# A two-level fast matrix product on one core: x loaded as fp16 by casting transfers from GpSimd, and one pair of additions moved to GpSimd

## The chip, the core and the metric

The kernel runs on one core of a Trainium2 chip. The core has five engines with instruction queues of their own: TensorE (PE, with its weight loads listed apart as PEld), VectorE (DVE), ScalarE (ACT), GpSimd (POOL) and SyncE (SP), which here only starts transfers. Each engine works through its queue strictly in order, and waits at an instruction until all that it depends on is done. The metric is the device time of the whole program in microseconds (us), median of the runs shown.

## The reference

```python
def reference(x, w):          # x: 8 x 2048 x 2048 float32, w: 2048 x 2048 float32
    cs = np.cumsum(x, axis=1)
    diff = cs - np.concatenate([zeros(8, 1, 2048), cs[:, :-1, :]], axis=1)
    return np.matmul(diff, w).astype(np.float32)
```

The difference of a running sum is x again, so what is computed is `x @ w`, with x seen as 16384 rows of 2048 numbers drawn from a normal distribution.

## The kernel before, in words

**Tiles and products.** The 128 row tiles of x (128 rows each) are numbered t. The first four (`PLAIN`) are multiplied in the plain way while w comes in. The others go in groups of four tiles, g to g+3 (g and h = g+2 give the upper blocks, g+1 and h+1 the lower ones), and a Strassen-like scheme with seven products instead of eight is used twice, one inside the other. w is held in SBUF as fp16 (its four blocks, and four combinations T1 to T4). There are 31 groups: `group_plain` for the first, `group` for the other thirty. A group's products are P1 and P2 (for C11), P5 (S1 with T1), the two direct ones `S2 T2` and `S3 T3`, which add up in the PSUM pairs X and Y, and P3 and P4. P1 to P5 are each split again into seven quarter products, `slot(0)` to `slot(6)` in the class `Quarters`. A quarter product needs sums of quarters of x: `s1`, `s2`, `s4` on DVE and `s3` on POOL. They are kept in two rooms, so `s3` overwrites `s1`, and has to wait until the product with `s1` (slot 1) is through. Slot 4 multiplies `s3`.

**How x comes in.** A tile comes as two halves of 128 x 1024 float32, by transfers that SP starts (`load`, L123) into four stage buffers F. ACT sums the magnitudes of each half (`weigh`, L133). From the two sums POOL makes the mean (L157), DVE its reciprocal (L159), and POOL the factor that undoes the scaling (`unit`, L160). ACT scales the halves to fp16 (`narrow`, L165), over the place of the first one. SP then starts two transposing transfers (`turn`, L185) into the x tiles that TensorE reads; a stage buffer is given back to the list after its narrow or its turn.

**How results go out.** ACT copies a PSUM bank into an SBUF buffer with the row's factor (`keep`, L561 to L568), DVE adds further banks to it (`add`, L573 to L579), and SP stores it (`put`, L582). X, once `S3 T3` is in it, goes into two results: `keep C21g` copies it, and `C22g+X` adds it to C22g, which already holds P5's part. The same holds for Y with C21h and C22h. Then P4 is added to C21 (`C21g+P4.g`, `C21h+P4.h`).

**What sets the order.** Every instruction is recorded with a label, an engine and a period (the group's number). The table `places` gives each label a due time inside its period of 2168 units, and `emit` (L197) issues all of them sorted by that time. So the table fixes the order of each engine's queue. Its entry `None` holds for the groups in the middle. In it, the end of a group has, in units: `keep C21g.0` 826, `keep C21g.1` 832, `C22g+X.0` 884, `keep C21h.0` 910, `C22h+Y.0` 989, `C22g+X.1` 990, `load8.0` 1057, `keep C21h.1` 1118, `load8.1` 1159, `C22h+Y.1` 1162, then the next group's `P1.s3` at 1213 (-955 of its own period) and `P2.s3` at 1426. `P4.s3` stands before them at 711, `load7.0` and `load7.1` at 790 and 818. ("load8" is the tile g+4 of the next group, by the number that it has in this one.)

Of the kernel before, what the change touches and what calls it, by code (L numbers as in the profile page):

```python
# [10 lines left out]
def kernel(  # L11
# [50 lines left out]
    tiny = const.tile([P, 64], f32, name="tiny")  # L62
    sums_at = [tiny[:, ds(2 * i, 2)] for i in range(4)]
# [14 lines left out]
    def area(kb, size, dtype):  # L78
        return arena[:, ds(kb * 256, size * 256)].bitcast(dtype) if dtype != f32 else arena[:, ds(kb * 256, size * 256)]
# [22 lines left out]
        last[engine] = said[-1] if isinstance(said, tuple) else said  # L102

    where = {}
    stage = [F[:, i, :] for i in range(4)]
    unit = {}
    sums_of = {}
    scales = {}
# [5 lines left out]
    def record(label, engine, ask):  # L114
        at = seen[period[0], label] = seen.get((period[0], label), 0) + 1
        if at > 1:
            label = f"{label}#{at}"
        ops.append((period[0], label, engine, ask))

    def role(t):  # L120
        return t - PLAIN - 4 * period[0]

    def load(t, i):  # L123
        if t < END:
            to = stage.pop(0)
            where.setdefault(t, [None, None])[i] = to
            record(
                f"load{role(t)}.{i}",
                "sp",
                lambda: nc.sync.dma_start(to, x2[ds(t * P, P), ds(i * NH, NH)]),  # L130
            )

    def weigh_one(t, i):  # L133
        m, data = sums_of[t][:, i : i + 1], where[t][i]
        record(
            f"weigh{role(t)}.{i}",
            "act",
            lambda: nc.scalar.activation(waste, data, ABS, scale=1.0 / ROW, accum_out=m),  # L138
        )

    def weigh(t, sides=range(2)):
        if t < END:
            if t not in sums_of:
                sums_of[t] = sums_at[t % 4]
            for i in sides:
                weigh_one(t, i)

    def scale_of(t):
        if t < END:
            m2 = sums_of.pop(t)  # L150
            m = means_at[t % 4]
            s = scales[t] = scales_at[t % 8]
            u = unit[t] = units_at[t % 8]
            record(
                f"mean{role(t)}",
                "pool",
                lambda: nc.gpsimd.tensor_scalar(m, m2[:, :1], m2[:, 1:], TINY, ADD, MAX),  # L157
            )
            record(f"scale{role(t)}", "dve", lambda: nc.vector.reciprocal(s, m))  # L159
            record(f"unit{role(t)}", "pool", lambda: nc.gpsimd.tensor_scalar(u, m, uw, None, MUL))  # L160

    def narrowed(t):
        return where[t][0].bitcast(f16)

    def narrow_one(t, i):  # L165
        to, data, s = narrowed(t)[:, ds(i * NH, NH)], where[t][i], scales[t]
        record(
            f"narrow{role(t)}.{i}",
            "act",
            lambda: nc.scalar.activation(to, data, COPY, scale=s),  # L170
        )
        if i == 1 and t != PLAIN + 1:
            stage.append(where[t][1])

    def narrow(t, sides=range(2)):
        if t < END:
            for i in sides:
                narrow_one(t, i)

    turns_left = {}  # L180

    def place(t):
        return turned_x[(t - PLAIN) // 2 % 2 + 2 * (t % 2)]

    def turn_one(t, i):  # L185
        to, data = place(t)[i], narrowed(t)[:, ds(i * NH, NH)]
        record(f"turn{role(t)}.{i}", "sp", lambda: nc.sync.dma_start_transpose(to, data))
        turns_left[t] = turns_left.get(t, 2) - 1
        if turns_left[t] == 0 and t != PLAIN + 1:
            stage.append(where[t][0])  # L190

    def turn(t, halves=range(2)):
        if t < END:
# [1 line left out]
                turn_one(t, i)  # L195

    def emit(places=None):  # L197
        def when(op):
# [254 lines left out]
    weigh(PLAIN + 2)  # L453
    scale_of(PLAIN + 2)
    finish_row(1)
    x5 = area(30, 8, f32)
    where[PLAIN + 1] = [x5[:, :NH], x5[:, NH:]]
    for i in range(2):

        def load_5(i=i):  # L460
            return nc.sync.dma_start(
                x5[:, ds(i * NH, NH)], x2[ds((PLAIN + 1) * P, P), ds(i * NH, NH)]
            )

        record(f"load1.{i}", "sp", load_5)
    put_done()
    narrow(PLAIN + 2)
    turn(PLAIN + 2)
# [292 lines left out]
    def group_plain(g):  # L761
        X, Y, Z, V = pairs
        h = g + 2
        ug, uh, vg = unit[g], unit[h], unit[g + 1]
        A11g, A12g = parts(g)
        A11h, A12h = parts(h)
        A21g, A22g = parts(g + 1)
# [24 lines left out]
        turn(h + 1)  # L792
        load(h + 4, 0)
        less("T2[4:]", T2[4:], B22[4:], T1[4:])
        vh = unit[h + 1]
# [88 lines left out]
    def group(g):  # L884
# [9 lines left out]
        ug, uh, vg, vh = (unit[t] for t in (g, h, g + 1, h + 1))  # L894
# [241 lines left out]
    period[0] += 1  # L1136
    ready["tail"]()


    places = {  # L1140
        0: {
# [493 lines left out]
    }  # L1635
    emit(places)


# [1 line left out]
_INS = ['x', 'w']  # L1640
# [26 lines left out]
```

## Time and profile before

| What | Value |
|---|---|
| median of two runs | 1456.43 us (1455.78 to 1457.09) |
| span of the profiled execution | 1457.7 us |
| DVE, ACT, POOL busy | 1245.1, 1132.1, 288.1 us |
| DMA share in the middle, 700 to 744 us | 0.88 |
| one load of 128 x 1024 float32, start to landing, median over the run | 5.5 us |
| one transposing transfer, the same | 3.7 us |

The profile gives the profiled execution its span, from the first to the last instruction, and no other time; the span is 1.27 us above the median of the runs. Engine rows of a timeline read: start, duration, engine, source line, operation, output <- inputs, count, and in brackets the idle time before it and what ended it. A line such as L520 is that of a helper and stands for many uses; the operands and the time tell them apart. Rows with SPq are transfers as SP issues them, not as they move.

### The profile page before, as it was taken

Reading aid. Unit: us, or ns where it says so; the run is one execution under the profiler, and the core shown is the slowest. Engines: PE = TensorE matmul, PEld = TensorE weight load, DVE = VectorE, ACT = ScalarE, POOL = GpSimd, SP = SyncE. Lnnn points to the kernel's source line nnn. Section 1 sums busy time; section 2 is a strip of 40 time slices with the busy share of each in tenths; the row PEclk is TensorE's granted clock in tenths of the full one; section 3 lists DMA queues with packets and bytes.
Section 4 is the critical chain, followed back from the end, with each engine's and each line's share of the span. In section 5 each row is a group of like instructions: output and inputs, shape, how many; then the busy total and the mean of one; then the engine's idle time right before and its main releaser. Section 6 shows DMA issues by size and latency. Waiting matters only on the chain.

```text
span 1457.7 us, 20733 instructions
## 1 busy us (share of the span) xinstructions
PE 1440.2 (99%) x6692; PEld 652.4 (45%) x6698; DVE 1245.1 (85%) x2075; ACT 1132.1 (78%) x1742; POOL 288.1 (20%) x400
## 2 busy tenths in 40 slices
PE   8999999999999999999999999999999999999998
PEld 3444444444444444444444444444444444444443
DVE  6998898888888888889888889888888888898887
ACT  5886678877788877788877788877788777788773
POOL 0001122212222212222122122122122122122211
PEclk9999999999999999999999999999999999999999
DMA  9999879999888999889998889998899999889983
GB/s 354 359 255 274 220 222 250 261 263 249 252 242 241 262 266 243 239 248 243 273 269 238 236 249 240 272 258 248 223 263 247 266 253 260 224 247 260 263 212 135
DMA packets 348108, 367.33 MB, mean 252 GB/s; under 512 B 271456, under 2 KB 271456, under 8 KB 348000
## 3 DMA queue, kind: packets, MB, share of 16 engines
q1 hardware_dynamic: 348000, 366.02, 89.3%
q8 instruction: 52, 0.85, 0.2%
q14 instruction: 56, 0.46, 0.1%
HBM read 166.20 MB, written 134.74 MB: 206 GB/s over the span
## 4 chain that ended last, share of the span: by engine, by line
PE 92%; DMA 5%; ACT 1%; issue 1%; DVE 0%; SPq 0%; DVEq 0%; POOL 0%; ACTq 0%
PE b L554 60%; PE b L532 32%; DMA W<-in_w_dram 2%; DMA W<-in_x_dram 2%; DMA out_dram<-arena 0%; DMA x<-arena 0%; DMA F<-in_x_dram 0%; ACT waste L138 0%; ACT arena L287 0%; ACT F L170 0%; DVE arena L579 0%; ACT arena L318 0%; ACT arena L568 0%; ACT W L417 0%; SPq L245 0%
## 5 line engine op out<-in xcount | busy, mean ns | idle before, releaser
L532 PE MATMUL b<-W,x 128*128 128x512 f16 x2176 | 523.2, 379 | 0.6 <-DMA x<-F 0.6
L579 DVE SCALAR_TENSOR_TENSOR arena<-b,tiny,arena 128x512 f32<-128x512 f32 x612 | 439.7, 743 | 55.4 <-ACT arena L568 42.8
L554 PEld LDWEIGHTS <-arena 128*128 128x128 f16 x2700 | 264.0, 98 | 321.3 <-issue 3.5
L554 PE MATMUL b<-W,arena 128*128 128x512 f16 x1640 | 405.6, 379 | 0.6 <-ACT arena L571 0.6
L568 ACT ACTIVATE arena<-b,tiny 128x512 f32<-128x512 f32 x496 | 322.3, 685 | 51.4 <-PE b L532 39.4
L532 PEld LDWEIGHTS <-x 128*128 128x128 f16 x2176 | 212.9, 98 | 257.5 <-DMA x<-F 1.1
L170 ACT ACTIVATE F<-F,tiny 128x1024 f16<-128x1024 f32 x246 | 282.0, 1147 | 52.0 <-DVE tiny L159 47.0
L554 PE MATMUL b<-W,x 128*128 128x512 f16 x1180 | 297.1, 379 | 0.0
L571 ACT COPY arena<-b 128x512 f32<-128x512 f32 x294 | 169.7, 586 | 147.5 <-PE b L554 136.8
L138 ACT ACTIVATE waste<-F 128x1024 uint8<-128x1024 f32 x246 | 260.2, 1058 | 13.5 <-DMA F<-in_x_dram 11.7
L554 PE MATMUL b<-arena 128*128 128x512 f16 x1060 | 266.9, 379 | 0.5 <-DVE tiny L159 0.3
L520 POOL TENSOR_TENSOR arena<-x,x 128x512 f16<-128x512 f16 x118 | 142.7, 1210 | 543.9 <-PE b L554 511.9
L520 DVE TENSOR_TENSOR b<-b,arena 128x512 f32<-128x512 f32 x294 | 203.2, 692 | 38.1 <-ACT arena L571 37.3
L554 PEld LDWEIGHTS <-x 128*128 128x128 f16 x1416 | 138.5, 98 | 167.4 <-issue 0.7
L520 DVE TENSOR_TENSOR arena<-W 128x2048 f16<-128x2048 f16 (+1 forms) x127 | 149.4, 1177 | 2.8 <-PE b L554 2.5
L157 POOL TENSOR_SCALAR tiny<-tiny 128x1 f32<-128x1 f32 x124 | 41.8, 337 | 439.3 <-ACT waste L138 414.3
L571 ACT COPY b<-b 128x512 f32<-128x512 f32 x147 | 85.0, 578 | 35.8 <-DVE arena L579 20.6
L520 DVE TENSOR_TENSOR arena<-x,arena 128x512 f16<-128x512 f16 x118 | 50.2, 427 | 54.3 <-PE b L554 54.3
L520 DVE TENSOR_TENSOR x<-x,x 128x1024 f16<-128x1024 f16 x124 | 82.3, 681 | 0.2
L520 DVE TENSOR_TENSOR arena<-W,arena 128x2048 f16<-128x2048 f16 (+1 forms) x70 | 75.3, 1076 | 3.1 <-PE b L554 3.0
L160 POOL TENSOR_SCALAR tiny<-tiny 128x1 f32<-128x1 f32 x124 | 72.1, 583 | 0.7
L554 PE MATMUL b<-arena,x 128*128 128x512 f16 x236 | 60.2, 379 | 0.0
(46 smaller groups left out, 616.4 us busy)
## 6 DMA issues: line engine op xcount, KB each, us to landing
F<-in_x_dram SPq DMA_DIRECT2D x246, 512.0 KB, 5.5
out_dram<-arena SPq DMA_DIRECT2D x240, 512.0 KB, 5.4
W<-in_w_dram SPq DMA_DIRECT2D x32, 512.0 KB, 9.0
arena<-kept SPq DMA_DIRECT2D x29, 512.0 KB, 4.4
out_dram<-arena SPq DMA_DIRECT2D x32, 256.0 KB, 2.9
W<-in_x_dram SPq DMA_DIRECT2D x16, 256.0 KB, 7.6
x<-F SPq DMA_TRANSPOSE x246, 3.7
arena<-in_x_dram SPq DMA_DIRECT2D x2, 512.0 KB, 4.7
```

The costliest lines, as they stand in the source:

```text
L138: lambda: nc.scalar.activation(waste, data, ABS, scale=1.0 / ROW, accum_out=m),
L157: lambda: nc.gpsimd.tensor_scalar(m, m2[:, :1], m2[:, 1:], TINY, ADD, MAX),
L160: record(f"unit{role(t)}", "pool", lambda: nc.gpsimd.tensor_scalar(u, m, uw, None, MUL))
L170: lambda: nc.scalar.activation(to, data, COPY, scale=s),
L520: record(label, engine, lambda: on.tensor_tensor(dst, p, q, op))
L532: said = nc.tensor.matmul(to[n], a[k], b[k][:, n, :], start=(start and k == 0), stop=(k == KH - 1), skip_group_check=True,)
L554: said = nc.tensor.matmul(to, a[k], b[k], start=(start and k == 0), stop=(k == 3), skip_group_check=True)
L568: record(label, "act", lambda: nc.scalar.activation(c, p, COPY, scale=u))
L571: record(label, "act", lambda: nc.scalar.copy(to, p))
L579: label, "dve", lambda: nc.vector.scalar_tensor_tensor(c, p, u, c, MUL, ADD)
```

## The change

- `load` asks for the transfer on GpSimd's queue, and the destination is fp16: the transfer casts. F has six fp16 buffers where it had four float32 ones. The two loads of the tile `PLAIN + 1` change in the same way. The engine field of these records is "pool", so they stand in POOL's queue at the due times that they had in SP's.
- `scale_of` and `narrow` do nothing any more. There are no means, reciprocals, factors by row or scaled copies; where a row's factor was used, w's own factor `uw` is.
- `weigh` stays on ACT and writes its sums to a table `told`, a column for each half.
- The additions `C22g+X` and `C22h+Y` read the SBUF copy (C21g, C21h) that `keep` has just made, in place of the PSUM banks, and run on POOL as plain tensor_tensor additions. `emit` sets each of the four at 0.5 units after its keep, and the store of the result not before them.
- In the last group's period six small instructions (`flag1` to `flag6`) ask whether all sums lie between 16 and 4000, four of them before and one after an all-reduce over partitions on POOL.
- After everything, each engine loads that flag into a register, and a branch holds a general kernel (w again, x row tile by row tile in a loop). It is taken only if a sum lies outside.

```diff
-    F = const.tile([P, 4, NH], f32, name="F")
+    F = const.tile([P, 6, NH], f16, name="F")
+    told = const.tile([P, 2, END - PLAIN], f32, name="told")
...
             record(
                 f"load{role(t)}.{i}",
-                "sp",
-                lambda: nc.sync.dma_start(to, x2[ds(t * P, P), ds(i * NH, NH)]),
+                "pool",
+                lambda: nc.gpsimd.dma_start(to, x2[ds(t * P, P), ds(i * NH, NH)]),
             )
 
     def weigh_one(t, i):
-        m, data = sums_of[t][:, i : i + 1], where[t][i]
+        m, data = told[:, i, ds(t - PLAIN, 1)], where[t][i]
...
-            lambda: nc.scalar.activation(waste, data, ABS, scale=1.0 / ROW, accum_out=m),
+            lambda: nc.scalar.activation(waste, data, ABS, accum_out=m),
...
     def scale_of(t):
-        if t < END:
...
-            record(f"scale{role(t)}", "dve", lambda: nc.vector.reciprocal(s, m))
-            record(f"unit{role(t)}", "pool", lambda: nc.gpsimd.tensor_scalar(u, m, uw, None, MUL))
+        pass
...
     def narrow(t, sides=range(2)):
-        if t < END:
-            for i in sides:
-                narrow_one(t, i)
+        pass
...
     def turn_one(t, i):
-        to, data = place(t)[i], narrowed(t)[:, ds(i * NH, NH)]
+        to, data = place(t)[i], where[t][i]
         record(f"turn{role(t)}.{i}", "sp", lambda: nc.sync.dma_start_transpose(to, data))
-        turns_left[t] = turns_left.get(t, 2) - 1
-        if turns_left[t] == 0 and t != PLAIN + 1:
-            stage.append(where[t][0])
+        if t != PLAIN + 1:
+            stage.append(data)
...
     def emit(places=None):
+        for own in places.values():
+            for a, b in (("C22g+X", "keep C21g"), ("C22h+Y", "keep C21h")):
+                for n in range(2):
+                    if f"{b}.{n}" in own:
+                        own[f"{a}.{n}"] = own[f"{b}.{n}"] + 0.5
...
-        add("C22g+X", C22g, X, vg, [1])
         keep("keep C21g", X, vg, C21g, [1])
-        add("C22g+X", C22g, X, vg, [0])
+        for n in (1, 0):
+            tensor(f"C22g+X.{n}", C22g[:, n, :], C22g[:, n, :], C21g[:, n, :], ADD, "pool")
...
-        C21h = keep("keep C21h", Y, vh, halves=[0])
-        add("C22h+Y", C22h, Y, vh, [0])
-        keep("keep C21h", Y, vh, C21h, [1])
-        add("C22h+Y", C22h, Y, vh, [1])
+        C21h = keep("keep C21h", Y, vh)
+        for n in range(2):
+            tensor(f"C22h+Y.{n}", C22h[:, n, :], C22h[:, n, :], C21h[:, n, :], ADD, "pool")
...
+    def judge():
+        record("flag1", "dve", lambda: nc.vector.tensor_scalar(fits, told, 4000.0, None, IS_LE))
...
+    judge()
...
     emit(places)
 
+    v = nc.values_load(fault[0:1, 0:1], min_val=0, max_val=1)
+    with tc.If(v > 0):
+        for ko in range(KO):
...
+            nc.sync.dma_start(out2[ds(i * P, P), :], c)
```

More of the change, by code (lines that the diff above doesn't have):

```diff
@@ L104 @@
     where = {}
-    stage = [F[:, i, :] for i in range(4)]
+    stage = [F[:, i, :] for i in range(6)]
     unit = {}
@@ L197, in emit @@
     def emit(places=None):
+        for own in places.values():
[3 more added lines that the diff above has]
+                        own[f"{a}.{n}"] = own[f"{b}.{n}"] + 0.5
+            for t in "13":
+                for label in (f"put{t}.1", f"put{t}.1.0", f"put{t}.1.1"):
+                    if label in own:
+                        name = {"1": "C22g+X", "3": "C22h+Y"}[t]
+                        halves = label[-1] if label.count(".") == 2 else "01"
+                        own[label] = max([own[label]] + [own[f"{name}.{n}"] + 0.2 for n in halves if f"{name}.{n}" in own])
         def when(op):
@@ L455 @@
     finish_row(1)
-    x5 = area(30, 8, f32)
-    where[PLAIN + 1] = [x5[:, :NH], x5[:, NH:]]
+    x5 = area(30, 8, f16)
+    where[PLAIN + 1] = [x5[:, :NH], x5[:, 2 * NH : 3 * NH]]
     for i in range(2):
         def load_5(i=i):
-            return nc.sync.dma_start(
-                x5[:, ds(i * NH, NH)], x2[ds((PLAIN + 1) * P, P), ds(i * NH, NH)]
+            return nc.gpsimd.dma_start(
+                where[PLAIN + 1][i], x2[ds((PLAIN + 1) * P, P), ds(i * NH, NH)]
             )
-        record(f"load1.{i}", "sp", load_5)
+        record(f"load1.{i}", "pool", load_5)
     put_done()
@@ L893, in group @@
         S2g, S2h, S3g, S3h, S4g, S4h = A11g, A11h, A21g, A21h, A12g, A12h
-        ug, uh, vg, vh = (unit[t] for t in (g, h, g + 1, h + 1))
+        ug = uh = vg = vh = uw
         next_g, next_h, next_k, next_l = g + 4, h + 4, g + 5, h + 5
@@ L1636 @@
     emit(places)
+    v = nc.values_load(fault[0:1, 0:1], min_val=0, max_val=1)
+    with tc.If(v > 0):
+        for ko in range(KO):
+            k = ko % KH
+            raw = W[k][:, 2 * NH :]
+            to = W[k].bitcast(f16)[:, ds(ko // KH * N, N)]
+            nc.sync.dma_start(raw, w[ds(ko * P, P), :])
+            nc.scalar.activation(to, raw, COPY, scale=uinv)
+        xs = area(0, 8, f32)
+        xn = area(8, 4, f16)
+        c = area(16, 8, f32)
+        xt = turned_x[0]
+        sums, mean, s, u = tiny[:, 0:2], tiny[:, 8:9], tiny[:, 9:10], tiny[:, 13:14]
+        with tc.For_i(0, M // P, 1) as i:
+            nc.sync.dma_start(xs, x2[ds(i * P, P), :])
+            for a in range(2):
+                nc.scalar.activation(
+                    waste, xs[:, ds(a * NH, NH)], ABS, scale=1.0 / ROW, accum_out=sums[:, a : a + 1]
+                )
+            nc.vector.tensor_scalar(mean, sums[:, :1], sums[:, 1:], TINY, ADD, MAX)
+            nc.vector.reciprocal(s, mean)
+            nc.vector.tensor_scalar(u, mean, uw, None, MUL)
+            nc.scalar.activation(xn, xs, COPY, scale=s)
+            for a in range(2):
+                nc.sync.dma_start_transpose(xt[a], xn[:, ds(a * NH, NH)])
+            for n in range(4):
+                for ko in range(KO):
+                    nc.tensor.matmul(
+                        banks[n],
+                        xt[ko // KH][:, ko % KH, :],
+                        W[ko % KH].bitcast(f16)[:, ds(ko // KH * N + n * NB, NB)],
+                        start=(ko == 0),
+                        stop=(ko == KO - 1),
+                    )
+                nc.scalar.activation(c[:, ds(n * NB, NB)], banks[n], COPY, scale=u)
+            nc.sync.dma_start(out2[ds(i * P, P), :], c)
 _INS = ['x', 'w']
```

56 lines of the change are left out of this document (31 added, 25 removed).

## The prediction

> **What bounds the kernel now.** I read the page's first line and busy shares, then the chain that ended last, then a table by stage.
>
> ```profile
> span 1457.7 us, 20733 instructions
> PE 1440.2 (99%) x6692; PEld 652.4 (45%) x6698; DVE 1245.1 (85%) x2075; ACT 1132.1 (78%) x1742; POOL 288.1 (20%) x400
> ...
> PE 92%; DMA 5%; ACT 1%; issue 1%; DVE 0%; SPq 0%; DVEq 0%; POOL 0%; ACTq 0%
> ```
>
> TensorE is busy for all but 17.5 us (1457.7 - 1440.2), and 92% of the last chain is TensorE. The stages say where those 17.5 us lie:
>
> ```profile
> core 0: us, PE busy (x) PEld busy (x) DVE busy (x) ACT busy (x) POOL busy (x), PEclk, DMA share, GB/s
> 0.00:10.00 10.00, 4.83 (x15) 1.83 (x16) 3.90 (x10) 2.33 (x2) 0.19 (x4) 1.00 0.75 220
> 10.00:55.00 45.00, 43.00 (x239) 20.91 (x243) 36.95 (x38) 34.03 (x39) 0.00 (x0) 1.00 1.03 406
> 55.00:101.00 46.00, 42.54 (x195) 18.89 (x195) 41.41 (x68) 39.92 (x56) 3.74 (x10) 1.00 0.97 275
> 700.00:744.03 44.03, 44.03 (x205) 19.97 (x204) 37.60 (x64) 35.26 (x55) 9.31 (x13) 1.00 0.88 253
> 1414.00:1458.00 44.00, 37.98 (x176) 17.01 (x174) 33.32 (x52) 18.89 (x32) 7.27 (x7) 0.97 0.39 132
> ```
>
> The head loses 5.2 + 2.0 + 3.5 us, the end 6.0. A group in the middle (44.03 us) loses nothing: 44.03 busy of 44.03 at a granted clock of 1.00. The change leaves every matmul as it is, so in some 30 groups there is nothing to win, whatever it takes off DVE and ACT. What it can win is a part of the head; what it can lose is a stall in each group, times 28 or so.
>
> **Part by part: what is taken off.** One group in the middle, by groups of instructions between 700 and 744.03 us:
>
> ```profile
> L579 DVE SCALAR_TENSOR_TENSOR arena<-b,tiny,arena 128x512 f32<-128x512 f32 x21 | 15.1, 742 | 1.8 <-ACT arena L568 1.6
> L170 ACT ACTIVATE F<-F,tiny 128x1024 f16<-128x1024 f32 x8 | 9.2, 1147 | 1.6 <-DVE tiny L159 1.4
> L520 POOL TENSOR_TENSOR arena<-x,x 128x512 f16<-128x512 f16 x4 | 4.6, 1162 | 19.4 <-PE b L554 19.4
> L160 POOL TENSOR_SCALAR tiny<-tiny 128x1 f32<-128x1 f32 x4 | 2.4, 599 | 0.0
> L157 POOL TENSOR_SCALAR tiny<-tiny 128x1 f32<-128x1 f32 x4 | 1.2, 298 | 11.6 <-ACT waste L138 11.6
> L159 DVE RECIPROCAL tiny<-tiny 128x1 f32<-128x1 f32 x4 | 0.6, 158 | 1.1 <-POOL tiny L157 1.1
> ```
>
> ACT loses eight narrows, 9.2 us. DVE loses four additions at 742 ns (3.0 us) and the reciprocals (0.6). POOL loses 3.6 us of tiny work. All of it lies beside a full TensorE: gain 0. `weigh` stays, and I leave its price as it is. The transposes wait for one step less, so SP is earlier, not later.
>
> **What is put on POOL.** Per group four additions of 128x512 with two SBUF inputs, which I price at the 1.16 us of POOL's own sums above (same count of elements, though fp16): 4.6 us; and eight issues of a casting load. With the five sums left POOL has 5.8 + 4.6 + 8L of 44.03 us, where L is what one issue holds POOL for. So the load on it is no matter below L = 4.2; its order is. By the due times the queue after `P4.s3` is: `load7.0`, `load7.1`, the two `C22g+X`, `C22h+Y.0`, `load8.0`, `C22h+Y.1`, `load8.1`, `P1.s3`, `P2.s3`. The same place in the trace, rows of the timeline by engine:
>
> ```profile
> 735.23 1.16 POOL L520 TENSOR_TENSOR arena<-x,x 128x512 f16<-128x512 f16 x1 [0.30 <-PE b L554]
> 749.04 1.16 POOL L520 TENSOR_TENSOR arena<-x,x 128x512 f16<-128x512 f16 x1 [12.65 <-PE b L554]
> ...
> 741.03 1.26 ACT L568 ACTIVATE arena<-b,tiny 128x512 f32<-128x512 f32 x2
> 742.95 0.69 ACT L568 ACTIVATE arena<-b,tiny 128x512 f32<-128x512 f32 x1 [0.66 <-PE b L532]
> 746.40 0.69 ACT L568 ACTIVATE arena<-b,tiny 128x512 f32<-128x512 f32 x1 [0.65 <-PE b L532]
> ...
> 750.30 0.75 PEld L554 LDWEIGHTS <-arena 128*128 128x128 f16 x4
> ```
>
> 735.23 is `P4.s3`, 749.04 is `P1.s3`, which waits for TensorE (its room) and ends at 750.20; the weight load of `P1.4`, its reader, comes at 750.30. So `P1.s3` has 0.10 us of slack. The gap of 12.65 us ahead of it looks wide, but it isn't free to be used: `C22h+Y.1` cannot start before `keep C21h.1`, the ACT row at 746.40, which itself waits for TensorE, and both it and `load8.1` stand before `P1.s3`. The sum: 746.40 + 0.69 (keep) + 1.16 (addition) + L + 1.16 (`P1.s3`) = 749.41 + L, with some 0.05 for the hand-overs 749.46 + L, against 750.30. TensorE stalls in each group by s = L - 0.84, if that is positive. The next group has the same sum again, as all of it hangs on TensorE's own progress.
>
> **L** isn't in the trace. The nearest rows are SP's issues:
>
> ```profile
> 734.77 0.53 SPq L587 DMA_DIRECT2D out_dram<-arena  x1
> 737.21 0.34 SPq L587 DMA_DIRECT2D out_dram<-arena  x1
> 722.63 1.23 SPq L187 DMA_TRANSPOSE x<-F  x1
> ```
>
> A store is issued in 0.34 to 0.53 us, a transposing transfer with its many small pieces in 1.23. I take L = 1.0, nearer to the upper one, as POOL does by program what SP does by a unit; ends 0.34 and, if it is held (below), 2.2. The Trainium skill (DMA: Bandwidth & Descriptors, "Latency and other measured facts") gives about 1 us to the first byte on GpSimd's path and 0.6 on the other; no run here shows it, and the sum would stay where it is.
>
> **A second price: the port.** Does POOL's work get in DVE's way?
>
> ```profile
> 728.58 1.52 POOL L160 TENSOR_SCALAR tiny<-tiny 128x1 f32<-128x1 f32 x1
> ...
> 728.27 0.62 DVE L520 TENSOR_TENSOR arena<-arena,x 128x512 f16<-128x512 f16 x1
> 728.81 1.21 DVE L520 TENSOR_TENSOR arena<-W 128x2048 f16<-128x2048 f16 x1
> 747.84 0.41 DVE L520 TENSOR_TENSOR arena<-x,arena 128x512 f16<-128x512 f16 x1
> ```
>
> Yes: the tiny POOL operation, 298 ns at best, took 1.52 us and ended with DVE's 1.21 us one; and DVE's 0.41 us operation took 0.62 while a POOL sum ended. One holds the other off for its whole length. Just as `C22h+Y.1` becomes ready (747.1) DVE has the 0.41 us operation of the row at 747.84, which comes earlier as the addition ahead of it is gone: either may be first. I add 0.2 (0 to 0.41). So s = 1.0 - 0.84 + 0.2 = 0.36 us, times 28 groups with a `load8.1`: **10.1 us**, 0 if L is 0.34, and 18 at L = 1.23 with 0.25 for the port.
>
> The other additions: `C22g+X` read what the keeps at 741.03 leave, and `C21g+P4.g` on DVE must now wait until POOL has read C21g.
>
> ```profile
> 741.74 1.41 DVE L579 SCALAR_TENSOR_TENSOR arena<-b,tiny,arena 128x512 f32<-128x512 f32 x2 [0.93 <-ACT arena L568]
> 743.40 2.06 DVE L579 SCALAR_TENSOR_TENSOR arena<-b,tiny,arena 128x512 f32<-128x512 f32 x3
> ```
>
> With the narrow ahead gone, the keeps come about 1 us earlier, POOL's first addition ends near 742, and the second of the two at 741.74 (`C21g+P4.g.0`) starts no later than now: price 0. The cover is the room that the removed additions leave, one in the first row and two in the second, 2.2 us; if it is gone, `P1.s2` behind them is late by what is missing. Loads: by the table each wanted buffer was given to its turn 457 units (9.3 us) or more before; data are wanted 355 units (7.2 us) or more after the issue, and take 4.9 (row below). Price 0.
>
> **The DMA engines.** Answer for 700 to 744 us:
>
> ```profile
> q1 hardware_dynamic: 10922, 11.10, 87.9%
> ...
> F<-in_x_dram SPq DMA_DIRECT2D x8, 512.0 KB, 4.9
> ```
>
> A casting transfer reads the same 512 KB and writes half. No row has one. From below, written bytes count: a gain, hidden. From above, twice the time: 512 KB at 406 GB/s (the head's row) is 1.29 us, times eight 10.3 us more in a group, on 38.7 (0.879 x 44.03): 49.0, over the 44.03 there are. I take the same time as now, since the reading side doesn't change; price 0.
>
> **The head.** Rows of TensorE, and of the chain there:
>
> ```profile
> 73.11 1.02 PE L430 MATMUL b<-W,arena 128*128 128x512 f16 x4 [0.52 <-DVE W L415]
> 80.74 7.94 PE L532 MATMUL b<-W,x 128*128 128x512 f16 x36 [0.57 <-DMA x<-F]
> 90.95 3.63 PE L532 MATMUL b<-W,arena 128*128 128x512 f16 x16 [2.27 <-DVE arena L520]
> ...
> 78.44 5.58 DMA F<-in_x_dram
> 84.01 6.17 DMA x<-arena
> ```
>
> The last two stalls come from loads, weighing, narrowing and turns in one queue; without the narrows and with loads in a queue of their own they can go: -2.8 us, -3.4 with the first. Against it: `load0` and `load2` are POOL's first work, write to fresh buffers and wait for nothing. They leave at time 0, not behind all of w: 4 x 0.524 MB = 2.1 MB ahead of or among the first tiles, at 406 GB/s 5.2 us on a head whose DMA share is 1.03. Net **+1.8** (-3.4 to +5).
>
> **The end.** The last DVE addition and the stores behind it:
>
> ```profile
> 1452.34 1.40 DVE L579 SCALAR_TENSOR_TENSOR arena<-b,tiny,arena 128x512 f32<-128x512 f32 x2
> 1453.10 0.99 SPq L599 DMA_DIRECT2D out_dram<-arena  x2
> ...
> DMA to landing us min/median/max: 2.3/2.4/3.0
> ```
>
> The flags stand half a group before that, on engines with room: 0. The register loads and the branch come after each engine's last work, partly under the 2.4 us of the last stores. From 1456.5 (1453.10 + 0.99 + 2.4) to 1457.7 the program's closing already takes 1.2; I bound the branch by 0 and four such closings, 5, and take 2. The Trainium skill (Runtime: NRT & Kernel Launch, "Instruction fetch mechanics") warns that a taken branch to a page not at hand waits for a fetch from memory; no row here shows one, and it would lie inside that bound.
>
> **Sum**, against the profiled execution: 1457.7 + 10.1 + 1.8 + 2.0 = 1471.6; the median of the runs lies 1.27 below the span, so **1470 us**, 0.9% slower. What a measurement of this kernel tells from no change I put at 2%, 29 us.
>
> **Rivals.** *POOL held at its issues (other side, slower by over 2%).* Place: `load8.1`. If DVE's two-input operations keep POOL from writing, as in the row at 728.58, L grows by one 1.21 us operation to 2.2: s = 1.56, times 28 is 43.7 us, 1504 in all. It decides from s = 0.91, L = 1.55 with the port's 0.2. For it: the 1.52 us row, and that the slack of 0.10 us is so thin. Against: DVE's rows from 748.2 to 750.3 have one input in PSUM. The Trainium skill's page "SBUF — State Buffer" ("SBUF: two separate sides") speaks against the change: a transfer issued from GpSimd starves while DVE runs in a two-port mode, 620 ns becoming about 3100. By that L would be 3.1 and the total about 1530; its section "Who interferes with whom" excepts two-input tensor operations, and no run here shows such an issue. Chance 0.20.
>
> *Casting transfers are slow.* 49.0 us of transfers in a group of 44.03: 28 x 5.0 = 140, about 1600. Against: the share of 0.88 holds overlap (a share of 1.03 stands in the head), so doubled loads may still fit. Chance 0.07.
>
> *No stall at all.* L is 0.84 or less, the port is free, and the head gains its 3.4: 1453 to 1458. For it: SP's 0.34. Chance 0.17.
>
> *It doesn't do what it says:* the branch is taken. The sums are of 1024 normal magnitudes, near 817, between 16 and 4000: 0.
>
> **How the numbers follow.** Forecast 0.55, held 0.20, slow cast 0.07, no stall 0.17, 0.01 for a gain beyond the head's. The range takes in the no-stall case and s up to 1.36: 1452 to 1498; the rest of "held" and the slow cast, under 0.2, stay out. Within 2%: forecast and no stall, 0.72. Slower: 0.27. Faster by 29 us would need TensorE under its 1440 busy: 0.01.
>
> **What would show it.** Right: 0.2 to 0.5 us of PE idle before the weight load of `P1.4` in each group, ended by POOL; POOL's sum after an issue; the narrows gone and ACT near 26 us a group; first x tiles later; groups of 44.2 to 44.5 us. Wrong: PE idle with a DMA as releaser (slow cast), groups of 44.03 (no stall), over 45 (held), or a stall at another reader such as `P2.3`, which waits for DVE through `C21h+P4.h`.

## The result, and the profile after

The changed kernel takes 1559.38 us (median of two runs, 1559.15 to 1559.6) against 1456.43: a ratio of 1.069, interval 1.064 to 1.075. It is 7% slower, and above the predicted range (1452 to 1498 us). First the page of the changed kernel: its first line, the engines, the two queues of the transfers, and two rows of the transfers' issues (size, median us from issue to landing).

```profile
span 1557.4 us, 20445 instructions
PE 1466.5 (94%) x6692; PEld 656.0 (42%) x6698; DVE 1215.9 (78%) x1836; ACT 866.2 (56%) x1494; POOL 474.5 (30%) x521
...
q1 hardware_dynamic: 312288, 235.98, 58.1%
q0 software_dynamic: 35712, 65.03, 30.5%
...
F<-in_x_dram POOLq DMA_DIRECT2D x246, 256.0 KB, 6.7
...
x<-F SPq DMA_TRANSPOSE x246, 5.6
```

The work taken off is gone (ACT 1132.1 to 866.2 us, DVE 1245.1 to 1215.9), and the two queues together hold the DMA engines for 58.1 + 30.5 = 88.6% of the span, a little less than the one queue of before (89.3%). Yet a load lands 6.7 us after its issue (5.5 before), a transpose 5.6 (3.7 before). The changed kernel by stages: two of the head, and 400 us of the middle.

```profile
10.00:55.00 45.00, 41.07 (x214) 20.25 (x218) 32.72 (x36) 31.45 (x37) 0.00 (x0) 0.89 1.04 394
55.00:101.00 46.00, 45.89 (x213) 20.85 (x213) 44.75 (x66) 34.12 (x50) 13.36 (x11) 1.00 1.05 248
600.00:1000.00 400.00, 380.82 (x1741) 170.61 (x1740) 310.99 (x468) 226.29 (x401) 131.03 (x149) 0.99 0.94 194
```

The same 400 us of the kernel before:

```profile
600.00:1000.00 400.00, 400.00 (x1854) 181.28 (x1853) 342.11 (x573) 319.68 (x500) 84.57 (x119) 1.00 0.90 250
```

Before, TensorE was busy for 400.00 of 400 us; after, for 380.82. So the loss is in the groups of the middle. To divide it, I take an instruction that a group has once, GpSimd's sum of two fp16 tiles of the arena for P5 (29 in each timeline, so 28 groups from the first to the last); here are those two, before and after.

```profile
191.28 1.16 POOL L520 TENSOR_TENSOR arena<-arena 128x512 f16<-128x512 f16 x1
...
1426.15 1.16 POOL L520 TENSOR_TENSOR arena<-arena 128x512 f16<-128x512 f16 x1 [9.83 <-PE b L554]
```

```profile
195.25 2.01 POOL L502 TENSOR_TENSOR arena<-arena 128x512 f16<-128x512 f16 x1 [6.66 <-DVE arena L502]
...
1518.19 1.16 POOL L502 TENSOR_TENSOR arena<-arena 128x512 f16<-128x512 f16 x1 [10.90 <-PE b L536]
```

Of the 99.7 us between the spans the stretch up to the first mark (the head and the first groups) has 4.0 (195.25 - 191.28), the 28 groups between the marks 88.1 (1322.94 against 1234.87, 3.15 us each), and the end 7.7 (39.21 against 31.55). What ends TensorE's waits, and ACT's, over the whole run (us in total, times, longest):

```profile
ACT arena L550 <- DMA out_dram<-arena: 118.5, 24, 8.2
...
PE b L536 <- ACT b L553: 51.0, 27, 3.4
...
PE b L536 <- POOL arena L502: 5.4, 6, 2.3
```

In the kernel before, the only such wait of ACT for a store was 1.0 us, and TensorE did not wait for ACT's copies in PSUM (`b`) at all. Between the two marks TensorE is idle for 66.5 us, against 1.1 before, and 51.0 of them end with ACT's copy. For nearly the same count of products it is busy for 22.7 us longer (1256.47 against 1233.73), in part at a lower clock (below). Together these are the 88. One group shows the chain, as rows of the timeline of POOL, SP, ACT and PE:

```profile
737.11 1.16 POOL L502 TENSOR_TENSOR arena<-x,x 128x512 f16<-128x512 f16 x1 [6.62 <-PE b L536]
738.21 1.10 POOL L131 DMA_DIRECT2D F<-in_x_dram  x2
...
739.04 0.34 SPq L569 DMA_DIRECT2D out_dram<-arena  x1
...
748.49 0.69 ACT L550 ACTIVATE arena<-b,tiny 128x512 f32<-128x512 f32 x1 [5.35 <-DVE arena L502]
749.07 0.58 ACT L553 COPY arena<-b 128x512 f32<-128x512 f32 x1
749.54 0.60 ACT L553 COPY b<-b 128x512 f32<-128x512 f32 x1
...
750.19 1.02 PE L536 MATMUL b<-arena 128*128 128x512 f16 x4 [1.94 <-ACT b L553]
...
795.04 0.69 ACT L550 ACTIVATE arena<-b,tiny 128x512 f32<-128x512 f32 x1 [5.64 <-DMA out_dram<-arena]
```

The row at 739.04 is `put2.1`, the store of C12h's second half. `keep C21h.0` (748.49) takes over C12h's buffer, so it waits until that store has landed. The line of the store alone, after and then before, by its time from issue to landing:

```profile
L569 SPq DMA_DIRECT2D out_dram<-arena x1: 338/338/338, 739.0 to 739.0; - x1
...
DMA to landing us min/median/max: 9.3/9.3/9.3
```

```profile
L587 SPq DMA_DIRECT2D out_dram<-arena x1: 337/337/337, 737.2 to 737.2; - x1
...
DMA to landing us min/median/max: 5.1/5.1/5.1
```

Both stores are issued 1.9 to 2.0 us after `P4.s3` (737.11 and 735.23). Before, the store landed at 742.3 and `keep C21h.0` came at 742.95, held by TensorE: 0.6 us to spare in this group. After, it landed at 748.3 and the keep came at 748.49. (The row at 748.49 names DVE as its releaser, which had long been done; one group later, at 795.04, the same keep names the store.) Over the groups between 250 and 1250 us the median landing of `put2.1` is 4.3 us before, which leaves 1.4 us, and 9.4 after. Behind that keep in ACT's queue stand its two copies of 749.07 and 749.54, the second of which is `P1`'s first: TensorE waits for it, 1.94 us. What stands ahead of the store is the row at 738.21: `load7.0` and `load7.1` leave 0.8 us before `put2.1`. By the table they come later than it (790 and 818 against 654), and in the kernel before SP, which issues all three, did issue them 2.8 us behind it, at 740.03:

```profile
740.03 1.61 SPq L130 DMA_DIRECT2D F<-in_x_dram  x2
```

In GpSimd's queue nothing holds them. Where TensorE's wait for ACT's copy is longest, it costs twice. TensorE's row, and the stage that follows:

```profile
700.75 1.87 PE L536 MATMUL b<-arena 128*128 128x512 f16 x4 [3.44 <-ACT b L553]
```

```profile
700.70:706.00 5.30, 5.25 (x13) 1.87 (x13) 2.54 (x4) 3.28 (x6) 2.75 (x4) 0.50 0.98 238
```

After 3.44 us of idle the granted clock is 0.50 for these 5.3 us, and four products take 1.87 us in place of 1.03.

### The profile page after: what moved, and what is told of

It reads as the page before. It is cut to its first block, busy times and chain, and to the rows that moved or that the text cites. A ratio compares the mean times of both kernels' runs of the same rounds, so it can differ in the third digit from the quotient of the medians.

```text
span 1557.4 us, 20445 instructions
## 1 busy us (share of the span) xinstructions
PE 1466.5 (94%) x6692; PEld 656.0 (42%) x6698; DVE 1215.9 (78%) x1836; ACT 866.2 (56%) x1494; POOL 474.5 (30%) x521
## 3 DMA queue, kind: packets, MB, share of 16 engines
q1 hardware_dynamic: 312288, 235.98, 58.1%
q0 software_dynamic: 35712, 65.03, 30.5%
## 5 line engine op out<-in xcount | busy, mean ns | idle before, releaser
L550 ACT ACTIVATE arena<-b,tiny 128x512 f32<-128x512 f32 x496 | 318.7, 689 | 234.2 <-DMA out_dram<-arena 118.5
L561 DVE SCALAR_TENSOR_TENSOR arena<-b,tiny,arena 128x512 f32<-128x512 f32 x492 | 354.5, 744 | 63.3 <-PE b L536 34.5
L536 PE MATMUL b<-arena 128*128 128x512 f16 x1060 | 273.8, 386 | 56.9 <-ACT b L553 49.5
L502 POOL TENSOR_TENSOR arena<-arena 128x512 f32<-128x512 f32 (+1 forms) x149 | 188.7, 1273 | 444.5 <-ACT arena L550 216.1
L502 POOL TENSOR_TENSOR arena<-x,x 128x512 f16<-128x512 f16 x118 | 147.5, 1250 | 502.5 <-PE b L536 455.8
L139 ACT ACTIVATE waste<-F 128x1024 uint8<-128x1024 f16 x246 | 260.6, 1059 | 11.4 <-DMA F<-in_x_dram 9.5
L502 DVE TENSOR_TENSOR arena<-x,arena 128x512 f16<-128x512 f16 x118 | 75.9, 644 | 127.5 <-PE b L536 127.5
L131 POOL DMA_DIRECT2D F<-in_x_dram x246 | 143.9, 587 | 60.8 <-DMA x<-F 38.5
L502 DVE TENSOR_TENSOR arena<-arena,x 128x512 f16<-128x512 f16 x118 | 75.4, 639 | 0.3
L502 DVE TENSOR_TENSOR arena<-x 128x512 f16<-128x512 f16 x118 | 54.5, 462 | 13.6 <-PE b L536 12.6
```

Of the source, the lines that this page charges most:

```text
L131: lambda: nc.gpsimd.dma_start(to, x2[ds(t * P, P), ds(i * NH, NH)]),
L139: lambda: nc.scalar.activation(waste, data, ABS, accum_out=m),
L502: record(label, engine, lambda: on.tensor_tensor(dst, p, q, op))
L536: said = nc.tensor.matmul(to, a[k], b[k], start=(start and k == 0), stop=(k == 3), skip_group_check=True)
L550: record(label, "act", lambda: nc.scalar.activation(c, p, COPY, scale=u))
L561: label, "dve", lambda: nc.vector.scalar_tensor_tensor(c, p, u, c, MUL, ADD)
```

## The experiments

Groups are measured as above; "middle" is TensorE's busy time in the 400 us from 600 to 1000. It understates a loss, since products at a lower clock count as busy, and short waits show in part only: the second row has 398.19, with groups that are 0.6 us longer. The last column is the median time of `put2.1` from issue to landing, in the groups between 250 and 1250 us (4.3 in the kernel before). All ratios stand against the kernel before, run beside them (1456 to 1462 us).

| Kernel | us | ratio (interval) | middle | `put2.1` lands |
|---|---|---|---|---|
| changed kernel | 1559.38 | 1.069 (1.064 to 1.075) | 380.82 | 9.4 |
| before, C22 additions on GpSimd alone | 1482.57 | 1.017 (1.014 to 1.019) | 398.19 | 4.6 |
| changed, C22 additions back on VectorE | 1562.14 | 1.069 (1.067 to 1.072) | 379.84 | 9.0 |
| changed, narrow fp16 loads from GpSimd | 1506.81 | 1.032 (1.031 to 1.034) | 393.00 | 7.2 |
| changed, narrow fp16 loads from SP | 1475.79 | 1.012 (1.010 to 1.014) | 399.32 | 4.4 |
| changed, no judging and no branch | 1540.92 | 1.058 (1.052 to 1.064) | 382.77 | 9.3 |
| changed, tile 7's loads and sums later | 1575.97 | 1.077 (1.074 to 1.081) | 377.48 | 4.7 |
| no judging, a fifth result buffer | 1499.15 | 1.027 (1.024 to 1.030) | 394.33 | 9.3 |
| that, with tile 7's loads and sums later | 1570.36 | 1.073 (1.069 to 1.077) | 380.53 | 4.7 |
| changed, tile 7's loads later, sums in narrow7's places | 1557.69 | 1.068 (1.065 to 1.071) | 386.45 | 4.6 |
| that, with the fifth buffer, no judging | 1550.97 | 1.061 (1.057 to 1.066) | 385.57 | 4.7 |
| no judging, fifth buffer, C22 on VectorE | 1492.72 | 1.021 (1.018 to 1.024) | 399.82 | 9.0 |
| before, float32 loads from GpSimd | 1638.75 | 1.121 (1.116 to 1.127) | 360.05 | 7.4 |
| changed, narrow bfloat16 loads from GpSimd, cast | 1514.52 | 1.038 (1.033 to 1.043) | 391.39 | 7.6 |

**The C22 additions alone, and taken back.** The kernel before with only this edit, and the changed kernel without it:

```diff
-        add("C22g+X", C22g, X, vg, [1])
         keep("keep C21g", X, vg, C21g, [1])
-        add("C22g+X", C22g, X, vg, [0])
+        for n in (1, 0):
+            tensor(f"C22g+X.{n}", C22g[:, n, :], C22g[:, n, :], C21g[:, n, :], ADD, "pool")
```

> The kernel before with only the four C22 additions moved to GpSimd (loads, scales and narrows as before, no judging). Theory 'additions': they hold GpSimd and then P1.s3, and cost most of the 3.15 us that a group grew by: about 1540 us. Theory 'transfers' (late landing of the store whose buffer the copy C21h.0 needs): the additions cost no more than the slack in front of P1.s3 allows, 0 to 0.3 us a group: 1455 to 1466 us, and the copy C21h.0 still waits for TensorE, not for a store.

> The changed kernel with the C22 additions back on VectorE as before; casting loads from GpSimd, no scales, judging and branch stay. Theory 'additions': back to about 1465 us. Theory 'transfers': nearly as slow as the changed kernel, 1545 to 1560 us, with ScalarE still waiting some 100 us in all for stores.

Alone they cost 22 us (1482.57 against 1460.25 beside it), 0.6 in a typical group (44.6 against 44.0), although no load is issued on GpSimd there. TensorE (matmuls, then weight loads) in one group of that kernel:

```profile
717.17 1.02 PE L566 MATMUL b<-W,x 128*128 128x512 f16 x4 [0.18 <-ACT b L583]
...
720.61 0.61 PEld L566 LDWEIGHTS <-arena 128*128 128x128 f16 x4 [0.32 <-POOL arena L532]
```

By the order of the queues the first is `P2.3`, through `C21h+P4.h` behind `C22h+Y.1` (the row itself names only ACT's copy); the second is the weights from `P2.s3`, as its releaser says. Neither theory had this size. Taking them back from the changed kernel gains nothing: 1562.14. ACT there waits for stores for 138.4 us, and GpSimd, with no additions between them, issues four loads in one go (739.58). So in the changed kernel their cost doesn't show beside the other wait.

**Queue, cast and bytes.** The loads read a narrow copy of x's first tile that lies in HBM as fp16, from GpSimd and then from SP; later a copy in bfloat16, which the transfer casts.

```diff
-                lambda: nc.gpsimd.dma_start(to, x2[ds(t * P, P), ds(i * NH, NH)]),
+                lambda: nc.gpsimd.dma_start(to, narrow_x[:, ds(i * NH, NH)]),
```

> The changed kernel with its loads from GpSimd's queue not casting: they read 128x1024 fp16 numbers (256 KB) from a narrow copy of the first row tile, which one casting transfer leaves in HBM at the start. Left out: the other row tiles' data; the product is of the first tile throughout. Theory 'cast' (the casting itself makes the transfers slow and holds the stores up): back to 1460 to 1475 us. Theory 'queue' (a ring of its own lets the loads past the store put2.1, whatever they carry): the store still lands late, above 1500 us.

> As the run without cast from GpSimd's queue, but the same narrow loads issued by SP at the same due times, so behind the stores in one ring. Left out: the other row tiles' data. Both theories: no stall from stores, groups of 44.0 to 44.4 us, 1455 to 1470 us. If it is slow as well, neither the cast nor the queue is the cause.

> The changed kernel with GpSimd's loads from a narrow copy of x's first tile in bfloat16, cast to fp16 by the transfer: the same 256 KB read and 256 KB written as in the run with fp16 loads from GpSimd without a cast (1506.8 us), but with the cast. It computes another product, as every tile of the groups is the first. Theory 'the cast': a casting transfer is slow in itself, whatever it reads, landing above 6 us, 1540 to 1565 us. Rival 'the bytes': the 52 us between that run and the changed kernel come from twice the bytes read, landing near 5.0 us, 1495 to 1520 us. Between the two, both have a part.

The loads' rows of the issues in these runs, in the order fp16 from GpSimd, fp16 from SP, bfloat16 cast by GpSimd:

```profile
F<-narrow_x POOLq DMA_DIRECT2D x246, 256.0 KB, 5.0
```

```profile
F<-narrow_x SPq DMA_DIRECT2D x246, 256.0 KB, 4.4
```

```profile
F<-narrow_x POOLq DMA_DIRECT2D x246, 256.0 KB, 4.9
```

With half the bytes read the changed kernel is 52.6 us faster, where theory 'queue' had it, and with SP's queue another 31.0 (1506.81 to 1475.79; groups of 44.2 us as expected, the total 6 us above its range). The cast by itself takes 1514.52 - 1506.81 = 7.7 us by the medians, with intervals that overlap, and the load with a cast lands no later than the one without (4.9 and 5.0 us): in the changed kernel it is not the cast that makes loads land late. That it is the 512 KB read is likely but not separated: these copies are one tile that is read again each time, so the place in HBM changed together with the bytes. ACT's waits for stores in these three runs:

```profile
ACT arena L555 <- DMA out_dram<-arena: 82.4, 23, 7.0
```

```profile
ACT arena L555 <- DMA out_dram<-arena: 17.8, 7, 4.9
```

```profile
ACT arena L555 <- DMA out_dram<-arena: 91.1, 26, 6.7
```

From SP the wait nearly goes, with the C22 additions, the judging and the branch all in place.

**The end.** Judging and branch are left out.

> The changed kernel without the judging and without the branch and the general kernel in it. Left out: the check of the sums; weighing stays. The last stretch, from P5's sum s3 of the last group to the end, grew from 31.55 to 39.21 us. Theory 'end': the all-reduce on GpSimd and the branch make these 7.7 us, so the time falls by 6 to 8 us to about 1552 us with the middle as slow as now. Rival: the end is long because its stores land late like the others: at most 2 us less.

The end falls from 39.2 to 32.0 us, as before (31.6). The rest of the 18 us that this kernel is faster lies in a middle that isn't the same from one profile to the next (46.75 us a group against 47.25), and I don't read it as an effect.

**One store, one buffer.** A fifth buffer for results, in the room that the judging leaves:

```diff
+    fifth = const.tile([P, 2, NB], f32, name="fifth")
...
+    free.append(fifth)
```

> The changed kernel without judging and branch (left out: the check of the sums, whose table shrinks) and with a fifth buffer for results, so that the copies C21g and C21h go into buffers whose stores were issued one store earlier. Theory 'one wait' (the wait of the copy C21h.0 for put2.1 is what costs): groups of 44.6 to 45.4 us, 1475 to 1500 us. Rival 'volume': the transfers are late as a whole and stop something else: groups of 46 us or more, above 1520 us.

41.8 us less than the same kernel without it (1540.92), just inside the range of 'one wait', and the wait of `keep C21h.0` is gone, although `put2.1` still lands after 9.3 us. Then, with the same buffer, the C22 additions back on VectorE:

> The kernel with the fifth result buffer, without judging and branch, and the C22 additions back on VectorE and PSUM as in the kernel before: only the casting loads on GpSimd and the missing scales are left of the change. Theory 'the additions cost 0.6 us a group, as alone in the kernel before': 1499 - 28 x 0.6 = 1482, 1474 to 1488 us. Rival 'they are paid only where nothing else is late, and the loads bunch more without them': 1492 to 1515 us.

By the total (1492.72) this lies at the lower edge of the rival's range, 5 us above the theory's. The middle says more (this kernel's profile is of its slowest execution, 1501.2 us); first with the additions on GpSimd, then without.

```profile
600.00:1000.00 400.00, 394.33 (x1809) 176.74 (x1808) 327.66 (x488) 236.76 (x418) 133.51 (x150) 1.00 0.94 198
```

```profile
600.00:1000.00 400.00, 399.82 (x1852) 180.87 (x1851) 342.74 (x537) 242.68 (x429) 90.93 (x118) 1.00 0.93 203
```

With both edits TensorE loses 0.18 us in 400, and a typical group takes 44.0 us: casting loads in GpSimd's queue then cost nothing there, at nearly the same DMA share of 0.93, and with `put2.1` still landing after 9.0 us. So the late store by itself costs nothing here; it costs where its buffer is wanted. The additions cost 0.3 us in a typical group of the other (44.3), of which a few groups take 45.6 to 47.3. What is left of this kernel's loss, against the kernel before, lies where the groups have tables of their own: 6.7 us in the head, 20 in the first three groups (151.1 against 131.2) and 11 in the last four (189.9 against 178.9).

**The loads behind, instead of a buffer.** `load7.0` and `load7.1` stand behind GpSimd's `C22g+X`, so that they leave after the store. First with the sums of tile 7 late (due 1560 and 1580), without and with the fifth buffer; then with the sums in the places of `narrow7`, as in this diff, again without and with it.

```diff
                         own[f"{a}.{n}"] = own[f"{b}.{n}"] + 0.5
+            if "C22g+X.0" in own and "load7.0" in own:
+                for n in range(2):
+                    own[f"load7.{n}"] = max(own["C22g+X.0"], own["C22g+X.1"]) + 0.1 + 0.1 * n
+                    own[f"weigh7.{n}"] = own.get(f"narrow7.{n}", own[f"weigh7.{n}"])
```

> The changed kernel with the two loads load7.0 and load7.1 behind the two C22g additions in GpSimd's queue (some 7 us later), so that the store put2.1 is through first, and the two weighings of that tile 7 to 8 us later. Theory 'collision' (these two casting loads share the DMA engines with put2.1, on whose landing the copy C21h.0 waits): put2.1 lands in about 5 us again, ScalarE's waits for stores all but vanish, groups of 44.6 to 45.4 us, 1480 to 1505 us. Rival 'volume' (casting loads take too much of the DMA engines wherever they stand): another store or turn is late instead, groups of 46 us and more, above 1525 us.

> Both of the last two together (later loads of that tile and a fifth buffer; left out: judging and branch). Theory 'collision' and 'one wait': nothing is left but the price of the C22 additions, 44.6 us a group as in the run with them alone, 1470 to 1485 us. Rival 'volume': above 1510 us.

> The changed kernel with load7.0 and load7.1 behind the two C22g additions in GpSimd's queue, as in the run that moved them and put the sums of tile 7 late, but with these sums now in the places that the removed narrows of tile 7 had, so that ScalarE no longer does four sums of magnitudes in a row ahead of P1's first copy. Theory 'passed store' (loads that leave ahead of one store delay it, and keep C21h.0 waits for its buffer): ScalarE's waits for stores at keep C21h.0 go, TensorE's waits for ScalarE's copies fall from 51 us to under 15, and the time is 1500 to 1530 us. Rival 'too much traffic' (whatever the order, a late transfer stalls some reader): 1545 us or more, with new waits for transfers.

> The same placement with the fifth result buffer, and without the judging and the branch (7 us less at the end). Theory 'passed store': both edits take away the same wait, so the time is that of the fifth buffer alone, 1499, within 12 us: 1487 to 1511 us. Rival 'too much traffic': over 1520 us. If each mends something of its own, under 1487 us.

In all four the theory missed, and the time lies in the range of the rival. But with `load7` behind it, `put2.1` lands after 4.6 to 4.7 us in all four, near the 4.3 of the kernel before. The line of the store in the third:

```profile
L573 SPq DMA_DIRECT2D out_dram<-arena x1: 338/338/338, 735.2 to 735.2; - x1
...
DMA to landing us min/median/max: 4.0/4.0/4.0
```

So it is these two loads ahead of it that make the store late. What was won there was lost elsewhere. In the first two I had put the sums of tile 7 next to those of the next tile. ACT in one group of the first, and TensorE behind it:

```profile
761.21 1.09 ACT L139 ACTIVATE waste<-F 128x1024 uint8<-128x1024 f16 x1
...
763.61 1.06 ACT L139 ACTIVATE waste<-F 128x1024 uint8<-128x1024 f16 x1
...
766.21 0.57 ACT L557 COPY b<-b 128x512 f32<-128x512 f32 x1 [0.30 <-DVE arena L565]
...
766.83 1.02 PE L540 MATMUL b<-arena 128*128 128x512 f16 x4 [1.81 <-ACT b L557]
```

The sums stand in a row, and the copy behind them is late by 1.81 us: a wait of my own making, in 25 groups (43.0 us). The third run has the sums apart. Its waits:

```profile
DVE arena L506 <- DMA x<-F: 43.9, 26, 9.0
...
ACT arena L554 <- DMA out_dram<-arena: 29.5, 23, 6.7
PE b L540 <- DVE arena L506: 27.1, 20, 4.3
...
PE b L540 <- ACT b L557: 8.1, 5, 3.8
```

The wait for ACT's copy fell as expected, from 51.0 to 8.1 us, and that for stores from 118.5 to 29.5. But x now comes late: DVE waits for transposes, and TensorE for DVE. The gain of the one is the loss of the other, with or without the fifth buffer (in the last of the four DVE waits 65.3 us for x). That moving the loads is enough is refuted: in the versions here they must leave as early as they do, and the store's buffer must not be needed. Nor does the rival hold in general, that a late transfer stalls some reader whatever the order: the kernel with the fifth buffer and the additions on VectorE has the same loads, and its middle loses next to nothing.

**The queue alone.** The kernel before, its float32 loads issued by GpSimd:

```diff
-                "sp",
-                lambda: nc.sync.dma_start(to, x2[ds(t * P, P), ds(i * NH, NH)]),
+                "pool",
+                lambda: nc.gpsimd.dma_start(to, x2[ds(t * P, P), ds(i * NH, NH)]),
```

> The kernel before with one part of the change alone: the float32 loads of the groups are issued by GpSimd in place of SP, at the same due times, with no cast, the same bytes, the same scales, narrows and additions. Theory 'order' (in a queue of their own loads leave as soon as a buffer is free, ahead of stores that stand before them by the table, and a late store holds keep C21h.0): ScalarE's waits for stores appear here too, and the time is 1480 to 1530 us. Rival 'cast' (the casting itself makes transfers late; a plain load from GpSimd is as good as one from SP): within 10 us of the kernel before, 1450 to 1470 us.

It is the slowest of all, by a wait that neither theory had. GpSimd in one group:

```profile
748.52 0.53 POOL L130 DMA_DIRECT2D F<-in_x_dram  x1 [14.53 <-DMA x<-F]
749.06 1.16 POOL L520 TENSOR_TENSOR arena<-x,x 128x512 f16<-128x512 f16 x1
```

With four stage buffers the load waits 14.53 us for a transpose to free one, and `P1.s3` stands behind it. TensorE's waits say what that costs:

```profile
PE b L554 <- POOL arena L520: 95.5, 23, 8.1
```
ACT's wait for stores is there too, 45.8 us in 20 waits, and `put2.1` lands after 7.4 us, with no cast. In the changed kernel, with six buffers, GpSimd's loads wait for transposes for 38.5 us in 6 waits, against 312.7 us in 44 here.

## Why the prediction was wrong, point by point

- **Nothing to win, whatever is taken off** (the steps "what bounds the kernel" and "what is taken off"): right. ACT is busy for 226.29 of 400 us in place of 319.68, and TensorE gained nothing by it.
- **"The DMA engines": price 0**, as the reading side doesn't change: the share came out near (0.94 after, 0.90 before; 88.6% of the span against 89.3%), but the conclusion was wrong. The step asked how long the engines are busy, not when one given transfer lands.
- **"Loads: price 0"** is the step that failed. It looked at the buffers that the loads want and at the data that they bring. It didn't ask what the loads pass: outside SP's queue, `load7` leaves ahead of `put2.1`, which lands after 9.4 us in place of 4.3 (medians). `keep C21h.0`, which needs that store's buffer, had 0.6 us to spare in the group shown; its row (742.95) stands in the prediction, the store's landing does not. The groups grew by 3.15 us each, where the prediction had 0.36, from a stall at another place.
- **The chain on GpSimd** (`C22h+Y.1`, `load8.1`, `P1.s3`): L measured 0.587 us, not 1.0, below the 0.84 that it decides at, and the additions 1.27, not 1.16. The rival "held" is out: the median issue took 0.57 us. The stall forecast there was mis-sized, then: L was 0.4 us too high and the addition 0.1 too low. By its own sum the chain then gives 746.40 + 0.69 + 1.27 + 0.59 + 1.16 = 750.11, with hand-overs and port 0.06 past its 750.30; the 0.6 us a group of the additions alone came at `P2.3` and `P2.s3`, the first of which the prediction named among the signs of its being wrong. The Trainium skill (SBUF — State Buffer, "Who interferes with whom") has two-input DVE operations hold off GpSimd's reads and not, as it infers, the writing of descriptors; the issues agree, at 0.57 us beside a DVE that is 78% busy.
- **The head**: right. By 101 us TensorE had begun 447 weight loads in place of 454, 7 fewer, which at 44.03 us for 204 of them is an estimated 1.5 us, against +1.8. The parts came out as well: 25 weight loads fewer from 10 to 55 us (218 in place of 243), about 5.4 us against 5.2, and 18 more from 55 to 101, about 3.9 us against 3.4. The loss goes with the early loads: by 55 us the run with GpSimd's queue alone had begun 238 weight loads, the one with the C22 additions alone 265, the kernel before 259. The other 2.5 us up to the first mark lie in the first groups.
- **The end**: "flags: 0" failed. Rows of GpSimd, DVE and TensorE in the last group of the changed kernel:

```profile
1525.57 0.38 POOL L1147 PARTITION_ALL_REDUCE tiny<-tiny  x1 [6.22 <-issue]
1532.95 1.14 POOL L502 TENSOR_TENSOR arena<-x,x 128x512 f16<-128x512 f16 x1 [7.01 <-DVE b L502]
...
1525.98 0.15 DVE L1151 CAST fault<-tiny 128x1 int32<-128x1 f32 x1 [2.62 <-POOL tiny L1147]
...
1526.52 1.04 PE L536 MATMUL b<-arena 128*128 128x512 f16 x4 [2.37 <-DVE arena L502]
...
1534.15 1.04 PE L536 MATMUL b<-arena 128*128 128x512 f16 x4 [2.29 <-POOL arena L502]
```

  The all-reduce takes 0.38 us, but 6.22 us pass before it and 7.01 after it, in which GpSimd computes nothing. DVE waits for it with a flag, and the sum behind it is late: 2.37 + 2.29 us of TensorE, together 4.7 of the 7.2 us by which the end is longer than without judging and branch. The branch was put at 2: from the last DVE addition to the end of the span 5.75 us pass, 4.40 in the run without judging and branch (3.95 in the kernel before), so flag loads and branch have about 1.35.
- **The rivals.** "Slow cast" named the nearest time, about 1600, for another reason: transfers that don't fit into a group. So its nearness is luck. They fit: with one more buffer, and the additions on VectorE, TensorE lost 0.18 us in 400 beside the same loads. And TensorE waited for a DMA by name only once, for 1.2 us; for the most part it waited for ACT, which waited for a store.

What stays open: why loads of 256 KB from GpSimd delay the store less than those of 512 KB (landing after 7.2 us in place of 9.4, waits of 82.4 us in place of 118.5), by their bytes or by the place that they read; and the 31 us in the first and last groups of the kernel with the fifth buffer and the additions on VectorE, whose own tables I didn't touch. No version here beats the kernel before: its middle groups have 44.0 us of TensorE in 44.0.

## What to carry to other kernels

When transfers move to another queue, ask not only what they wait for and who waits for them, but which transfers they will now pass, and how much slack the readers and the buffers of those have: in a tuned order a store with 0.6 us to spare can become part of the critical path. A share of busy DMA engines that stays the same says nothing of it. And before an edit is undone piece by piece, take away the one wait that the trace names: one buffer told more here than four changes of order.

## What the runs showed of the hardware beside this

- A casting load holds GpSimd for 0.57 us (median of 246), about as long as a plain one does in the kernel before with its queue changed (0.53, median).
- TensorE after 3.44 us of idle (700.75) ran at a granted clock of 0.50 for at least the 5.3 us shown, and after 1.94 us (750.19) at full speed (1.02 us for four products). The length of the wait alone doesn't decide it in this trace: after 2.51 us of idle (275.91) the mean clock was 0.58 over the next 4.1 us, after 2.67 us (417.41) it was 1.00 over 4.0. The Trainium skill (TensorE: Matmul & The Clock Gate, "Part 1: The HAM clock gate") puts the halving at an idle window of about 3.4 us; the row at 700.75 agrees, the one at 275.91, with less idle time, doesn't.
- GpSimd's all-reduce between tensor additions: 6.22 us ahead of it and 7.01 behind it without work. At the start of both gaps (1519.5 to 1519.6, and 1525.9) the trace has two instructions MODIFY_POOL_CONFIG of under 0.1 us. The Trainium skill (GPSIMD Engine Reference, "2.1 Instruction dispatch") gives the first call to freshly loaded code about 6 us that no instruction shows; the first gap agrees, with 6.0 us from the second of these instructions to the all-reduce. The second gap is a microsecond longer, and the addition at its end waited in it for a product of TensorE too (until 1527.6), so that the 7 us are not all a load of code.
